# Opening of a two-layer diffusion backbone kernel: conditions and x loaded first, x divided by its rms in place, modulation weights split by VectorE and GpSimd

## The chip, the core and the metric

The kernel runs on one NeuronCore of a Trainium2 chip. Time is device microseconds of one execution, and what is compared is the median of several runs. A profiled execution has a span of its own, from the first to the last instruction in the trace. Engines: TensorE (PE: matmuls; PEld: its weight loads), VectorE (DVE), ScalarE (ACT), GpSimd (POOL) and SyncE (SP), which issues most of the DMAs.

## The reference

```python
for l in range(DEPTH):                                    # 2 layers, D_MODEL = 1024
    sx1, cx1, gx1, sx2, cx2, gx2 = modulation(c, ada_w[l], ada_b[l])      # silu(c) @ w + b
    sc1, cc1, gc1, sc2, cc2, gc2 = modulation(c_ctx[None, :], ada_w[l], ada_b[l])
    hx = modulate(rms_norm(x, norm1_g[l]), sx1, cx1)      # h * (1 + scale) + shift
    hc = modulate(rms_norm(ctx, norm1_g[l]), sc1, cc1)
    zx = split_in(hx @ w_in[l])      # conv a, b | q, k, v | sgu u, v | gates
    ...                              # conv module, window attention, sgu, gated merge, w_o, conv FFN
```

x has 512 rows, ctx has 256, and both have 1024 features. Everything is float32, and the output is compared with a float32 reference.

## The kernel before

Activations are kept transposed: features on partitions, 768 tokens (512 of x, 256 of ctx) along the free axis, eight tiles of 128 features. To keep float32 precision on TensorE at a one-pass rate, an operand is split in two parts of the reduced type fp32r, `hi` (a rounded copy, made by ScalarE in `acopy`) and `lo` (the rest, subtracted by VectorE in `tt`), and a product is hi·hi + hi·lo + lo·hi: three matmuls (`linear_steps`). A plain fp32 matmul needs no split, and the trace shows it as two records.

The opening, up to the first of these products, does four things. (1) `load_cond` brings in c and c_ctx and applies SiLU. (2) `ada_start` computes what the first normalisation needs of the modulation of layer 0, 2048 columns, in two halves `g2`. A half reads 8 row tiles of 128 x 1024 (`k` = 0 to 7), each as two DMAs of 128 x 512; the 128 x 512 tile is the moving operand and the 4 columns of silu(c), silu(c_ctx) (hi and lo) are the stationary one. The result, 4 x 512 in two PSUM tiles `x`, is copied by ScalarE, turned to columns by 8 tiny matmuls against `sel`, and added to the bias into `mods`. Half 0 serves feature tiles 0 to 3, half 1 tiles 4 to 7. Five of the 16 row tiles go through TensorE as plain fp32, eleven are split. (3) `load_x` brings in x and ctx (tiles named g in the trace), four DMAs laid between the row tiles; `rms_sq` sums squares, `rstd_diag` gets 1/rms by a Newton iteration on 128 x 6 numbers and writes it on a diagonal, and `bcast_diag` spreads it over the partitions into PSUM tile `S`. (4) After both halves `norm_mod` makes the eight pairs (hi, lo) of the normalised input, tiles named h: a product with `S` on VectorE, scale and shift on ScalarE, hi and lo.

Then the main stream begins with the first 144 matmuls of layer 0, `ab(0)`: three token parts of 256, two weight tiles, eight feature tiles, three matmuls each. The next product begins with 128 x 512 matmuls.

What sets the order: the kernel is written against a framework that orders each engine's instructions when the program is built, by program order and by priorities (`tc.high_priority`); `paced` adds an order-only dependency on the last matmul noted in `last[0]`. On the chip each engine's queue is strictly in that order. Eight semaphores serve the DMAs in turn, so a DMA is issued only when the one eight places before it has landed.

Of the kernel before, what the change touches and what calls it, by code (L numbers as in the profile page):

```python
# [8 lines left out]
F32 = mybir.dt.float32  # L9
# [9 lines left out]
D = 1024  # L19
# [60 lines left out]
def body(tc, I, out):  # L80
# [136 lines left out]
    acopy(identr, msk[:, :128])  # L217
    acopy(maskb[:, 256:640], msk[:, 128:512])
# [60 lines left out]
    def load_cond():  # L279

        st = T(xp_, [128, 16], F32, "st", 1)
        rw = T(xp_, [2, 1024], F32, "rw", 1)
        nc.scalar.dma_start(out=st[:, :2 * KD], in_=I["ccol"])
        nc.scalar.dma_start(out=rw[:2], in_=I["crow"])
# [3 lines left out]
        act(out=rw[:2], in_=rw[:2], func=AF.Silu)  # L288
        V.memset(silf, 0.0)
        V.tensor_copy(out=silf[:, :, 0:2], in_=st[:, :2 * KD].rearrange("p (k c) -> p k c", c=2))  # L290
        split(silr[:, :, 0:2], silr[:, :, 2:4], silf[:, :, 0:2])
        tt(sel, ident[:4, 0:2], ident[:4, 2:4], add)
        nc.scalar.dma_start(out=sd, in_=rw[:2])

    def ada_start():

        for g2 in range(2):
            pm = [x_ps(), x_ps()]
            for k in range(KD):
                w = [(page("h", 16) if i else page("m", 8))[:, :512] for i in range(2)]  # L300
                for i in range(2):
                    nc.sync.dma_start(out=w[i], in_=I["ada0"][g2, k, :, i * 512:i * 512 + 512])
                for i in range(2):
                    if k < (3, 2)[g2]:
                        nc.tensor.matmul(pm[i][:4], silf[:, k, :], w[i], start=(k == 0), stop=(k == 7))
                        continue
                    hi = page("y", 8, F32R)[:, :512]
                    lo = T(sp, [128, CW0], F32R, "cy", 8)[:, :512]
                    split(hi, lo, w[i])
                    nc.tensor.matmul(pm[i][:4], silr[:, k, :], hi, start=(k == 0), stop=False)  # L310
                    nc.tensor.matmul(pm[i][:4], silr[:, k, :], lo, start=False, stop=(k == 7))
                yield
            with tc.high_priority(offset=600):
                pt = c_ps()
                for i, g in enumerate((g2, g2 + 2)):
                    r = page("t", NTP)[:4, :512]
                    acopy(r, pm[i][:4])
                    for j in range(4):
                        c = (i * 4 + j) * 2
                        nc.tensor.matmul(pt[:, c:c + 2], r[:, j * 128:j * 128 + 128], sel, start=True, stop=True)  # L320
                pv = pt[:, :16].rearrange("p (j c) -> p j c", c=2)
                for c in range(2):
                    for i, g in enumerate((g2, g2 + 2)):
                        tt(mods[0][c][:, g * 4:g * 4 + 4], pv[:, i * 4:i * 4 + 4, c], adab[0][:, g * 4:g * 4 + 4], add)
            yield
# [134 lines left out]
    def linear_steps(res, w, cs, hs, segs, k0=0):  # L460
# [3 lines left out]
        for o, n, c in segs:  # L464
            p = acc_ps(c)[:, :n]
            for k in range(nk):
                hi, lo = hs[k0 + k]
                nc.tensor.matmul(p, w[0][:, k, cs], hi[:, o:o + n], start=(k == 0), stop=False)  # L468
# [65 lines left out]

    load_cond()
    fvs[0] = load_fv(0)
    ag = ada_start()

    def ada_steps(n):
        for _ in range(n):  # L540
            next(ag, None)

    ada_steps(4)
    xs = load_x(lambda i: ada_steps(2))
# [4 lines left out]
    with tc.high_priority(offset=1000):  # L549
        bcast_rstd(acc, 0, NT, 1.0 / D, bx)  # L550
    ada_steps(99)
    px.close()
    hs = h_pages()
    for c in range(2):
        a1 = mod_scale(0, c, 1, FV_N1)
        for o, n, c_ in parts_of(True):
            if c_ == c:
                norm_mod(xs, bx[:, o:o + n], hs, o, n, a1, mods[0][c][:, 0:8])

    for l in range(2):  # L560
# [78 lines left out]
        def ab(i, w, t, sg_):  # L639
            for p, o, n, c in linear(w[0], slice(0, 128), hs, sg_):  # L640
                with evac():
                    act(out=t[:, o:o + n], in_=p, func=AF.Copy)
            for p, o, n, c in linear(w[1], slice(0, 128), hs, sg_):
# [5 lines left out]
        def ab_load(i):  # L649
            if i == 0 and full:  # L650
                ab_load.raw = [raw_tile() for _ in range(2)]
                for h in range(2):
                    for b in range(2):
                        nc.sync.dma_start(
                            out=ab_load.raw[b].rearrange("p (k c) -> p k c", k=8)[:, :, h * 128:h * 128 + 128],
                            in_=I["w_in"][l, :, b * 512 + h * 128:b * 512 + h * 128 + 128].rearrange("(k p) c -> p k c", p=128))
# [598 lines left out]
```

## Time and profile before

| what | us |
|---|---|
| median of 3 runs | 2097.68 (2093.98 to 2099.98) |
| profiled execution, its time | 2097.33 |
| profiled execution, its span | 2095.5 |
| TensorE busy in the span | 2050.4 (98%) |
| first matmul of the main stream | 51.43 |
| first 128 x 512 matmul behind the first product | 72.64 |

The page gives busy time by engine, the costliest groups of instructions and the DMAs. The views by stretch (windows) and in order of time (timeline) are read for the first 80 us and at the border between the layers. A row of the timeline has its start, its length, the engine and line, output and inputs, their shape, the count of instructions merged in it and, in brackets, the idle time before it and what ended that.

### The profile page before, as it was taken

How to read it: one execution, taken by the hardware profiler on the slowest of the kernel's cores; microseconds unless marked ns; L12 is line 12 of the kernel's file. 1: busy time of each engine (PE TensorE's matmuls, PEld its weight loads, DVE VectorE, ACT ScalarE, POOL GpSimd, SP SyncE). 2: the span in 40 equal slices, each digit the busy share in tenths (PEclk: the TensorE clock that was granted, in tenths of full speed). 3: DMA queues.
4: the chain of work that ended last, by engine and by line, in shares of the span. 5: the costliest groups of instructions: out<-in, count | busy, mean ns of one | idle time of the engine just before them, and what ended most of it. 6: DMA issues, size and time to landing. Idle time of an engine off the chain costs nothing.

```text
span 2095.5 us, 29640 instructions
## 1 busy us (share of the span) xinstructions
PE 2050.4 (98%) x11628; PEld 1769.3 (84%) x11628; DVE 1564.9 (75%) x3134; ACT 894.4 (43%) x1485; POOL 10.6 (1%) x24
## 2 busy tenths in 40 slices
PE   6999999999999899999999999999999999999999
PEld 2888898888878898888888898879888888888887
DVE  5689888888667778867595768998987467655654
ACT  5532235677523453323232325433687335333331
POOL 0000000000000000000000000000000000000000
PEclk9999999999999999999999999999999999999999
DMA  8121112213576133444343422322212432222321
GB/s 279 57 81 61 61 61 76 86 55 105 153 220 203 65 101 124 139 141 150 102 141 101 161 78 91 121 65 77 75 46 63 124 126 93 89 92 96 106 99 62
DMA packets 160468, 221.39 MB, mean 106 GB/s; under 512 B 7364, under 2 KB 102340, under 8 KB 160328
## 3 DMA queue, kind: packets, MB, share of 16 engines
q1 hardware_dynamic: 155712, 212.89, 31.5%
q10 hardware_dynamic: 4616, 6.61, 1.0%
q8 instruction: 91, 1.49, 0.3%
q14 instruction: 49, 0.40, 0.1%
HBM read 215.27 MB, written 4.20 MB: 105 GB/s over the span
## 4 chain that ended last, share of the span: by engine, by line
PE 59%; DVE 7%; DMA 4%; ACT 2%; issue 1%; SPq 0%; ACTq 0%; DVEq 0%
PE x L469 8%; PE x L468 8%; PE x L470 8%; PE b L469 7%; PE b L468 7%; PE b L470 7%; DMA t<-in_adat 2%; DVE cy L120 2%; DVE hl L117 2%; PE S L470 2%; PE S L468 2%; PE S L469 2%; PE c L470 2%; PE c L469 2%; PE c L468 2%
## 5 line engine op out<-in xcount | busy, mean ns | idle before, releaser
L114 ACT ACTIVATE hl<-raw 128x1024 fp32r<-128x1024 f32 x264 | 279.2, 1059 | 497.9 <-PE c L469 184.4
L117 DVE TENSOR_TENSOR hl<-raw,hl 128x1024 fp32r<-128x1024 f32 x264 | 322.5, 1222 | 158.8 <-ACT hl L114 156.0
L468 PE MATMUL x<-h,hl 128*128 128x512 f32 (+1 forms) x760 | 292.7, 387 | 6.6 <-ACT h L114 6.6
L470 PE MATMUL x<-h,hl 128*128 128x512 f32 (+1 forms) x760 | 291.7, 385 | 1.4 <-DVE hl L117 1.4
L469 PE MATMUL x<-h,hl 128*128 128x512 f32 (+1 forms) x760 | 292.6, 386 | 0.0
L120 DVE SCALAR_TENSOR_TENSOR cy<-cy,fv 128x503 f32<-128x503 f32 (+29 forms) x240 | 208.5, 880 | 3.0
L469 PE MATMUL b<-h,hl 128*128 128x512 f32 (+1 forms) x552 | 203.9, 370 | 0.0
L468 PE MATMUL b<-h,hl 128*128 128x512 f32 (+1 forms) x552 | 203.5, 370 | 0.0
L470 PE MATMUL b<-h,hl 128*128 128x512 f32 (+1 forms) x552 | 203.2, 369 | 0.3 <-DVE hl L117 0.3
L468 PEld LDWEIGHTS x<-h,hl 128*128 128x128 f32 x760 | 145.3, 192 | 31.0 <-ACT h L114 7.3
L470 PEld LDWEIGHTS x<-h,hl 128*128 128x128 f32 x760 | 145.5, 192 | 27.7 <-DVE hl L117 2.4
L469 PEld LDWEIGHTS x<-h,hl 128*128 128x128 f32 x760 | 145.9, 192 | 23.4 <-DVE h L117 0.3
L470 PEld LDWEIGHTS b<-h,hl 128*128 128x128 f32 x552 | 104.2, 189 | 18.1 <-DVE hl L117 0.7
L468 PEld LDWEIGHTS b<-h,hl 128*128 128x128 f32 x552 | 104.2, 189 | 17.0
L469 PEld LDWEIGHTS b<-h,hl 128*128 128x128 f32 x552 | 104.2, 189 | 16.4
L468 PE MATMUL c<-h,hl 128*128 128x256 f32 x400 | 112.7, 282 | 0.1
L469 PE MATMUL c<-h,hl 128*128 128x256 f32 x400 | 112.5, 281 | 0.1
L470 PE MATMUL c<-h,hl 128*128 128x256 f32 x400 | 112.5, 281 | 0.0
L120 DVE SCALAR_TENSOR_TENSOR m<-b,ff,m 128x511 f32<-128x511 f32 (+2 forms) x118 | 80.8, 688 | 36.1 <-ACT m L1128 34.6
L114 ACT ACTIVATE y<-m 128x512 fp32r<-128x512 f32 (+1 forms) x51 | 36.4, 713 | 128.3 <-DVE m L117 121.8
L468 PE MATMUL b<-y,hl 128*128 128x512 f32 (+1 forms) x256 | 86.3, 338 | 0.7 <-ACT y L114 0.7
L470 PE MATMUL b<-y,hl 128*128 128x512 f32 (+1 forms) x256 | 85.8, 335 | 0.0
(338 smaller groups left out, 4983.0 us busy)
## 6 DMA issues: line engine op xcount, KB each, us to landing
t<-in_adat SPq DMA_DIRECT2D x200, 256.0 KB, 3.4
raw<-in_w_in SPq DMA_DIRECT2D x44, 1024.0 KB, 5.3
raw<-in_ffn_up SPq DMA_DIRECT2D x44, 1024.0 KB, 5.1
raw<-in_ffn_down SPq DMA_DIRECT2D x22, 1024.0 KB, 5.1
raw<-in_w_o SPq DMA_DIRECT2D x8, 1024.0 KB, 7.3
g<-in_xt SPq DMA_DIRECT2D x8, 768.0 KB, 5.5
m<-in_ada SPq DMA_DIRECT2D x16, 256.0 KB, 5.4
h<-in_ada SPq DMA_DIRECT2D x16, 256.0 KB, 5.8
```

The lines of the kernel that those rows point to most:

```text
L114: act(out=o, in_=i, func=AF.Copy)
L117: V.tensor_tensor(out=o, in0=a, in1=b, op=op)
L120: return V.scalar_tensor_tensor(out=o, in0=a, scalar=s, in1=b, op0=op0, op1=op1)
L468: nc.tensor.matmul(p, w[0][:, k, cs], hi[:, o:o + n], start=(k == 0), stop=False)
L469: nc.tensor.matmul(p, w[0][:, k, cs], lo[:, o:o + n], start=False, stop=False)
L470: last[0] = nc.tensor.matmul(p, w[1][:, k, cs], hi[:, o:o + n], start=False, stop=(k == nk - 1))
```

## The change

The conditions come over SP's queue ahead of all else and x right behind them, before any modulation weight. Each half (`ada_half`) still has 8 row tiles; two of half 0 (k = 0, 1) and three of half 1 (k = 5 to 7) are plain fp32. In a split, ScalarE makes hi as before, and lo is subtracted by VectorE for the left half of a row tile and by GpSimd for the right one. 1/rms is found while half 0 runs, its spreading stands behind row tile 4 of half 0, and x is multiplied by it in place, eight products of 128 x 768. With half 0 known, `scaled_tiles` makes feature tiles 0 to 3: hi and the full value each by an own ScalarE instruction from x, lo by VectorE. Tiles 4 to 7 follow half 1, with hi on ScalarE and the full value on VectorE. The first weights `w_in` (`raw0`) are requested behind all modulation weights, and `behind` (in both layers) holds the first product's matmuls behind the last matmul written before them.

```diff
-    def ada_start():
-        for g2 in range(2):
...
-                    if k < (3, 2)[g2]:
...
-                    split(hi, lo, w[i])
...
+        nc.sync.dma_start(out=st[:, :2 * KD], in_=I["ccol"])
+        nc.sync.dma_start(out=rw[:2], in_=I["crow"])
...
+    def ada_half(g2, between=None):
+        pm = [x_ps(), x_ps()]
+        cyp = lambda: T(sp, [128, CW0], F32, "cy", 8)[:, :512]
+        src = [lambda: page("m", 8)[:, :512], lambda: page("y", 8)[:, :512], cyp, lambda: page("m", 8)[:, :512]]
+        tag, bufs = (("h", 16), ("y", 8))[g2]
+        for k in range(KD):
+            w = [src[g2 * 2 + k // 4]() for i in range(2)]
+            for i in range(2):
+                nc.sync.dma_start(out=w[i], in_=I["ada0"][g2, k, :, i * 512:i * 512 + 512])
+            for i in range(2):
+                if (k >= 5 if g2 else k < 2):
+                    last[0] = nc.tensor.matmul(pm[i][:4], silf[:, k, :], w[i], start=(k == 0), stop=(k == 7))
+                    continue
+                hi, lo = (page(tag, bufs, F32R)[:, :512] for _ in range(2))
+                acopy(hi, w[i])
+                (nc.gpsimd if i else V).tensor_tensor(out=lo, in0=w[i], in1=f(hi), op=sub)
+                nc.tensor.matmul(pm[i][:4], silr[:, k, :], hi, start=(k == 0), stop=False)
+                last[0] = nc.tensor.matmul(pm[i][:4], silr[:, k, :], lo, start=False, stop=(k == 7))
+            if between:
+                between(k)
...
+                stt(a1[c][:, v], mods[0][c][:, 8 + g2 * 4:12 + g2 * 4], 1.0, fvs[0][:, FV_N1 + g2 * 4:FV_N1 + g2 * 4 + 4], add, mul)
...
+                r = nc.tensor.matmul(p, w[0][:, k, cs], hi[:, o:o + n], start=(k == 0), stop=False)
+                if behind and k == 0:
+                    paced(r)
...
+    def scaled_tiles(js, o, n, c):
+        v = slice(o, o + n)
+        for j in js:
+            hi, lo = hs[j]
+            t = page("t", NTP)
+            aff = dict(in_=xs[j][:, v], func=AF.Identity, scale=a1[c][:, j:j + 1], bias=mods[0][c][:, j:j + 1])
+            act(out=hi[:, v], **aff)
+            if j < 4:
+                act(out=t[:, :n], **aff)
+            else:
+                ts(t[:, :n], xs[j][:, v], a1[c][:, j:j + 1], mul, mods[0][c][:, j:j + 1], add)
+            tt(lo[:, v], t[:, :n], f(hi[:, v]), sub)
...
-    ada_steps(4)
-    xs = load_x(lambda i: ada_steps(2))
+    xs = load_x()
...
+        dg = rstd_diag(acc, 0, NT, 1.0 / D)
+    ada_half(0, lambda k: k == 4 and bcast_diag(dg, NT, bx))
+    for j in range(KD):
+        tt(xs[j], xs[j], bx[:, :NT], mul)
+    hs = h_pages()
+    scaled_tiles(range(4), 0, NX, 0)
+    ada_half(1)
+    raw0 = [raw_tile() for _ in range(2)]
...
+    scaled_tiles(range(4), NX, NC, 1)
+    for q in parts_of(True):
+        scaled_tiles(range(4, 8), *q)
     px.close()
-    hs = h_pages()
-    for c in range(2):
...
-                norm_mod(xs, bx[:, o:o + n], hs, o, n, a1, mods[0][c][:, 0:8])
```

ScalarE's queue before, at the end of half 1: the last copy of a modulation tile (y from h), the copies of the result (t from x), the split of the first weights (hl from raw), two small loads, and the first steps of the normalised input (t and h).

```order
L114 ACTIVATE y<-h 128x512
L114 ACTIVATE t<-x 4x512 x2
L114 ACTIVATE hl<-raw 128x1024 x2
L240 DMA lng<-in_sln 128x512
L240 DMA lnb<-in_sln 128x512
L452 ACTIVATE t<-t,mod_85,a_429 128x256 x2
L114 ACTIVATE h<-t 128x256
```

The modulation came first, the weight split and the normalised input behind it. ScalarE's queue now, from half 0's result (t from x) over the making of feature tiles 0 to 3 (h and t from g) into half 1 (y from cy):

```order
L114 ACTIVATE t<-x 4x512 x2
L549 ACTIVATE h<-g_110,mod_83,a_108 128x512
L551 ACTIVATE t<-g_110,mod_83,a_108 128x512 x2
L551 ACTIVATE t<-g_111,mod_83,a_108 128x512 x2
L549 ACTIVATE h<-g_110,mod_84,a_109 128x256
L549 ACTIVATE h<-g_110,mod_83,a_108 128x512
L114 ACTIVATE y<-cy 128x512
L549 ACTIVATE h<-g_111,mod_83,a_108 128x512
L114 ACTIVATE y<-cy 128x512
```

and the end of the same queue's half 1:

```order
L549 ACTIVATE h<-g_111,mod_84,a_109 128x256
L114 ACTIVATE y<-cy 128x512
L114 ACTIVATE hl<-raw 128x1024
L114 ACTIVATE y<-cy 128x512
L114 ACTIVATE hl<-raw 128x1024
L114 ACTIVATE y<-m 128x512 x2
L114 ACTIVATE t<-x 4x512 x2
```

Twelve instructions on feature tiles 0 to 3 and the two weight splits now stand ahead of the last copies of half 1.

TensorE's queue before, from the last split tile (x from cy) over the result of half 1 (c from sel) and the spreading of 1/rms (S) to the first main matmuls (x and b from h and hl):

```order
L311 MATMUL x<-cy,silr 4x512
L320 MATMUL c<-sel,t 128x2 x4
L435 MATMUL S<-t,ones 128x512
L435 MATMUL S<-t,ones 128x256
L320 MATMUL c<-sel,t 128x2 x4
L468 MATMUL x<-h,hl 128x256
```

and now, from the end of half 1 (split tiles of y, plain tiles of m) to the first main matmuls (x from h and hl):

```order
L313 MATMUL x<-y,silr 4x512 x2
L314 MATMUL x<-y,silr 4x512
L308 MATMUL x<-m,silf 4x512
L314 MATMUL x<-y,silr 4x512
L308 MATMUL x<-m,silf 4x512 x5
L324 MATMUL c<-sel,t 128x2 x4
L473 MATMUL x<-h,hl 128x256
```

The six plain tiles of half 1 stand behind its last split tile, where plain tiles were the first of each half, and S is spread earlier, within half 0.

## Rows read from the trace of the kernel before

**Rows 1.** The page: busy time of TensorE, its share of the span and its instructions.

```profile
PE 2050.4 (98%) x11628; PEld 1769.3 (84%) x11628; DVE 1564.9 (75%) x3134; ACT 894.4 (43%) x1485; POOL 10.6 (1%) x24
```

**Rows 2.** Windows of 10 us: start and end, length, busy us of each engine (instructions), granted clock of TensorE, DMA share, GB/s.

```profile
0.00:10.00 10.00, 1.90 (x3) 0.35 (x4) 1.11 (x6) 4.56 (x7) 0.21 (x4) 1.00 0.82 256
10.00:20.00 10.00, 9.07 (x22) 1.79 (x20) 4.41 (x8) 3.78 (x6) 0.00 (x0) 1.00 1.00 363
20.00:30.00 10.00, 8.29 (x32) 2.82 (x32) 6.53 (x12) 8.94 (x13) 0.00 (x0) 1.00 1.04 400
30.00:40.00 10.00, 7.31 (x24) 3.56 (x25) 7.58 (x17) 7.42 (x14) 0.00 (x0) 0.70 1.10 335
```

**Rows 3.** Timeline of TensorE in the opening: plain fp32 tiles (L305), split tiles (L310, L311), sums of squares (L422), result of half 1, spreading of 1/rms (L435), main stream (L468 to L470).

```profile
9.76 1.91 PE L305 MATMUL x<-h,silf 128*4 128x512 f32 x2
11.46 1.91 PE L305 MATMUL x<-m,silf 128*4 128x512 f32 x2
...
18.06 0.40 PE L311 MATMUL x<-cy,silr 128*4 128x512 f32 x1
18.29 0.39 PE L310 MATMUL x<-y,silr 128*4 128x512 f32 x1
...
25.77 1.02 PE L305 MATMUL x<-m,silf 128*4 128x512 f32 x2
26.63 1.02 PE L305 MATMUL x<-h,silf 128*4 128x512 f32 x2
...
33.95 2.72 PE L422 MATMUL b<-ones,t 128*128 128x1 f32 x12
...
44.16 0.40 PE L311 MATMUL x<-cy,silr 128*4 128x512 f32 x1 [0.29 <-DVE cy L117]
...
45.47 1.56 PE L435 MATMUL S<-t,ones 128*128 128x512 f32 x4
...
51.43 0.58 PE L468 MATMUL x<-h,hl 128*128 128x256 f32 x1 [3.43 <-ACT h L114]
...
58.03 0.28 PE L470 MATMUL b<-h,hl 128*128 128x256 f32 x1
58.15 0.28 PE L468 MATMUL b<-h,hl 128*128 128x256 f32 x1
...
72.64 0.40 PE L468 MATMUL x<-h,hl 128*128 128x512 f32 x1
```

**Rows 4.** Timeline of ScalarE in the opening: squares (L414), hi copies and copies of the result (L114), scale and shift (L452).

```profile
25.15 3.90 ACT L414 ACTIVATE t<-g 128x768 f32<-128x768 f32 x5
...
34.20 0.62 ACT L114 ACTIVATE y<-m 128x512 fp32r<-128x512 f32 x1
34.72 0.61 ACT L114 ACTIVATE y<-h 128x512 fp32r<-128x512 f32 x1
...
43.67 0.59 ACT L114 ACTIVATE t<-x 4x512 f32<-4x512 f32 x1 [4.81 <-PE x L311]
...
45.09 1.99 ACT L114 ACTIVATE hl<-raw 128x1024 fp32r<-128x1024 f32 x2
...
51.29 0.58 ACT L452 ACTIVATE t<-t,mod,a 128x256 f32<-128x256 f32 x1
51.78 0.40 ACT L114 ACTIVATE h<-t 128x256 fp32r<-128x256 f32 x1
52.09 0.59 ACT L452 ACTIVATE t<-t,mod,a 128x256 f32<-128x256 f32 x1
```

**Rows 5.** Timeline of VectorE: lo subtraction of a modulation tile and the small step behind it, the diagonal of 1/rms, the lo of the first weights, the additions into mods, the product with S; then, at the border between the layers, the first step of the Newton iteration on 128 x 2 numbers and the diagonal that follows it.

```profile
38.22 0.68 DVE L117 TENSOR_TENSOR cy<-m,y 128x512 fp32r<-128x512 f32 x1
38.82 0.15 DVE L117 TENSOR_TENSOR nut<-nyt 128x6 f32<-128x6 f32 x1
...
44.02 0.95 DVE L117 TENSOR_TENSOR t<-identr,nyt 128x768 f32<-128x768 f32 x1
...
46.16 1.23 DVE L117 TENSOR_TENSOR hl<-raw,hl 128x1024 fp32r<-128x1024 f32 x1 [1.09 <-ACT hl L114]
48.04 0.37 DVE L117 TENSOR_TENSOR mod<-c,adab 128x4 f32<-128x4 f32 x4 [0.65 <-PE c L320]
...
49.53 1.41 DVE L117 TENSOR_TENSOR t<-g,S 128x256 f32<-128x256 f32 x4
...
1267.75 0.16 DVE L126 TENSOR_SCALAR nvt<-b 128x2 f32<-128x2 f32 x1 [0.30 <-PE b L422]
...
1270.72 0.42 DVE L117 TENSOR_TENSOR t<-identr,nyt 128x256 f32<-128x256 f32 x1
```

**Rows 6.** Windows of 1 us, TensorE alone: busy us (instructions), granted clock, DMA share, GB/s.

```profile
40.00:41.00 1.00, 1.00 (x4) 0.63 1.06 295
...
50.00:51.00 1.00, 0.00 (x0) 0.99 0.92 289
...
57.00:58.00 1.00, 1.00 (x7) 0.59 0.00 0
```

**Rows 7.** DMA issues of the first 80 us: the first weights, with count, KB each, median us from issue to landing.

```profile
raw<-in_w_in SPq DMA_DIRECT2D x4, 512.0 KB, 7.7
```

**Rows 8.** Timeline of TensorE at the border between the layers.

```profile
1264.26 0.39 PE L470 MATMUL x<-h,hl 128*128 128x256 f32 x1 [0.87 <-DVE hl L117]
```

**Rows 9.** GpSimd's groups by shape: its memsets of 64 x 512.

```profile
L915 POOL MEMSET qT<- 64x512 f32 x20 | 10.4, 521 | 1569.7 <-PE b L732 892.6 <-PE b L731 236.8 <-PE S L940 181.4
```

More of the change, by code (lines that the diff above doesn't have):

```diff
@@ L291, in load_cond @@
         split(silr[:, :, 0:2], silr[:, :, 2:4], silf[:, :, 0:2])
+        act(out=rw[:2], in_=rw[:2], func=AF.Silu)
+        nc.scalar.dma_start(out=sd, in_=rw[:2])
+        acopy(identr, msk[:, :128])
+        acopy(maskb[:, 256:640], msk[:, 128:512])
         tt(sel, ident[:4, 0:2], ident[:4, 2:4], add)
-        nc.scalar.dma_start(out=sd, in_=rw[:2])
-    def ada_start():
-        for g2 in range(2):
[L298 to L303, printed above, removed]
-                    if k < (3, 2)[g2]:
[L305 to L308, printed above, removed]
-                    split(hi, lo, w[i])
[L310 to L314, printed above, removed]
-                for i, g in enumerate((g2, g2 + 2)):
[L316 to L321, printed above, removed]
-                for c in range(2):
-                    for i, g in enumerate((g2, g2 + 2)):
-                        tt(mods[0][c][:, g * 4:g * 4 + 4], pv[:, i * 4:i * 4 + 4, c], adab[0][:, g * 4:g * 4 + 4], add)
-            yield
@@ new lines, in ada_half @@
+    def ada_half(g2, between=None):
[18 more added lines that the diff above has]
+                between(k)
+        with tc.high_priority(offset=600):
+            pt = c_ps()
+            for i, g in enumerate((g2, g2 + 2)):
+                r = page("t", NTP)[:4, :512]
+                acopy(r, pm[i][:4])
+                for j in range(4):
+                    c = (i * 4 + j) * 2
+                    nc.tensor.matmul(pt[:, c:c + 2], r[:, j * 128:j * 128 + 128], sel, start=True, stop=True)
+            pv = pt[:, :16].rearrange("p (j c) -> p j c", c=2)
+            for c in range(2):
+                for i, g in enumerate((g2, g2 + 2)):
+                    tt(mods[0][c][:, g * 4:g * 4 + 4], pv[:, i * 4:i * 4 + 4, c], adab[0][:, g * 4:g * 4 + 4], add)
+                v = slice(g2 * 4, g2 * 4 + 4)
+                stt(a1[c][:, v], mods[0][c][:, 8 + g2 * 4:12 + g2 * 4], 1.0, fvs[0][:, FV_N1 + g2 * 4:FV_N1 + g2 * 4 + 4], add, mul)
@@ L458, in norm_mod, with linear_steps @@
             tt(lo[:, v], t[:, :n], f(hi[:, v]), sub)
-    def linear_steps(res, w, cs, hs, segs, k0=0):
+    def linear_steps(res, w, cs, hs, segs, k0=0, behind=False):
         nk = w[0].shape[1]
@@ L533, in load_x @@
         return [xs[j // 2][:, (j % 2) * 768:(j % 2) * 768 + 768] for j in range(8)]
+    def scaled_tiles(js, o, n, c):
[10 more added lines that the diff above has]
+            tt(lo[:, v], t[:, :n], f(hi[:, v]), sub)
     load_cond()
     fvs[0] = load_fv(0)
[L537 to L541, printed above, removed]
-    ada_steps(4)
-    xs = load_x(lambda i: ada_steps(2))
+    a1 = [T(cp, [128, 8], F32, "a0%d1" % c, 1) for c in range(2)]
+    xs = load_x()
     acc = page("t", NTP)
@@ L650, in ab_load @@
             if i == 0 and full:
[L651 to L656, printed above, removed]
+                ab_load.raw = raw0
             elif i % 2 == 0:
```

21 lines of the change are left out of this document (7 added, 14 removed).

## The prediction

> **What bounds the kernel now.** The page first: TensorE is busy for 98% of the span [rows 1], so nearly all that is left to win lies where it isn't dense, and the windows show that this is the opening [rows 2]. The timeline of TensorE gives the two marks [rows 3]: the main stream starts at 51.43 and its first product ends at 72.64, where the 128 x 512 matmuls begin. From there the queues are the same before and after except at the layer border, and TensorE sets the pace. So the change is worth what it moves the 72.64, plus the border. The opening ended with half 1: its last lo matmul at 44.16, then the result, S, and the normalised input; the stream's first matmul waited 3.43 us for ScalarE's h [rows 3].
>
> **The change, step by step.** It adds and removes hardly any matmuls (ten plain tiles either way), so what counts is which queue is last. I follow the chain in the new order with durations from rows; all new clock times are estimates.
>
> *x lands, about 13.2.* x is 3.15 MB and 0.4 MB of small loads travel with it. By 10 us 2.56 MB had moved (256 GB/s), the next stretch ran at 363 [rows 2]; with a part of the next tile on the way that is 3.7 MB, 13.2. At 400 GB/s throughout it would be 11.5, with a slower start 14.
>
> *1/rms, about 22.9.* A square takes 0.78 (3.90 for five) [rows 4]: two remain after the last x tile, 14.8; the last addition, a 128 x 768 like the diagonal, 0.95 [rows 5], with hand-over 16.0. Six fp32 matmuls took 2.72 at the lower clock [rows 3]: 18.7. The Newton chain took 2.97 at the border (1267.75 to 1270.72), with one foreign instruction in it as now [rows 5]: with a slightly longer one 21.9. Diagonal 0.95: 22.9.
>
> *S, about 27.0.* The spreading stands behind three plain tiles and six split ones. A plain tile takes 0.86 at 2.4 GHz (25.77 to 26.63) and 1.70 at half of it (9.76 to 11.46) [rows 3]; I take 4.1 for three (bounds 2.6 and 5.1): 22.8. Six split tiles of two matmuls at 0.23 (18.06 to 18.29) [rows 3]: 25.6. The spreading took 1.56 [rows 3]: 27.0.
>
> *Half 0 known, about 32.9.* VectorE multiplies x by S. Four 128 x 256 took 1.41 [rows 5], 0.35 each, so 0.88 for 768 columns; between the first two pieces stand two lo of 0.60 (38.22 to 38.82) [rows 5]. The last lo is done at 30.0, TensorE at 30.6, two copies of 0.59 [rows 4], eight tiny matmuls and the additions (0.37 for four) [rows 5]: 32.9. This hides nothing and is hidden by nothing: ScalarE has run dry by then.
>
> *ScalarE's queue, 14.2 us.* From here to the last hi of half 1 the queue holds, in order, work of three kinds. Scale and shift on 256 columns is followed after 0.49 (51.29 to 51.78), a plain copy on 256 after 0.31 (51.78 to 52.09), one on 512 after 0.52 (34.20 to 34.72) [rows 4]; so scale and shift on 512 is 0.70. Eight of these (hi and full value of four tiles) 5.6; four on ctx 2.0; nine copies of modulation tiles 4.7; two weight splits, 1.99 together [rows 4]. Sum 14.2, end 47.1. The transfers don't hold it: by the rates of [rows 2] the modulation has landed near 35 and the first half of the weights (7.7 us from issue) [rows 7] near 38. VectorE runs beside it and ends with the second weight lo (1.23) [rows 5] and the last modulation lo: 48.0. GpSimd's last subtraction ends about there. No row shows a two-operand GpSimd instruction; its one-output memset of half the partitions takes 0.52 [rows 9], and three streams at that rate would be 1.56. I take 1.1, between them; at either end it is covered by the plain tile ahead of its matmul.
>
> The Trainium skill, GPSIMD Engine Reference, section Performance versus the Vector engine, gives 4497 ns for a two-operand instruction of 2048 columns; a quarter of it, 1.1 us, is an estimate for 512. The sum would not move by it.
>
> *Six plain tiles at the end, about 8.* Before, plain tiles led each half. Now all six of half 1 are behind the last split tile. At 2.4 GHz they take 5.2, at 1.2 GHz 10.2. TensorE was granted half its clock when it had idled 3.4 us before the main stream, from 51.0 to 57.6 [rows 3, 6], and in the new order it has only some 18 short matmuls between 32 and 48, so I take about 6 us at the lower clock: 8.0. With the last lo matmul, half 1 is through at 56.3, against 44.6 before.
>
> *From there to the end of the first product, 24.5.* Before it was 28.1 (44.6 to 72.64). Feature tiles 0 to 3 are ready now. The result takes two copies, the tiny matmuls and the additions, 2.1; ScalarE first makes four full values of ctx (2.0), then two hi for each tile, 0.98 a tile: VectorE has the fourth lo of the first part at 7.2. By then 24 of 144 matmuls are done; 120 at 0.12 (58.03 to 58.15) [rows 3] are 14.4. A gap of 5 us with little work costs the clock again, some 2.9. Bounds 21.6 and 27. End 80.8.
>
> *Sum.* 80.8 against 72.64 is +8.2. At the layer border the first product's matmuls no longer run ahead of their weights' lo, a wait of 0.87 [rows 8], and nothing is late in its place: −0.9. Span 2095.5 + 7.3 = 2102.8. The profiled execution's time was 1.8 above its span and 0.35 under the median of 2097.68: 2105.
>
> **Rivals.** *The transfers end it.* If half 0's result reached ScalarE by 26 us in place of 32.9, the queue would wait for weights at the end, not work. Then: weights near 38.2, split and two copies 2.0, GpSimd 1.1, plain tiles at the full clock 5.2, 21.6 more: 68.1, −4.5 − 0.9, 2092. For it speaks that 400 GB/s are seen from 20 us on [rows 2]; against it, that with each step of the 1/rms chain at its lower bound I get only to 28.7. This is the case on the other side; its deciding point is that 26 us.
>
> *The clock stays up.* The same chain to 48.0, but the plain tiles at 2.4 GHz (53.6) and no second loss (21.6): 75.2, +2.6 − 0.9, 2099.4. For it: 0.23 matmuls with waits between them ran at the full clock from 16 to 24 [rows 3]. Against: the idle before 51.43 cost it, and the new queue is emptier.
>
> *VectorE and GpSimd hold each other up.* Five subtractions of half 1 run while VectorE does nearly nothing but two-operand instructions. If each waits for the other, 1.1 to 1.56 five times, less 1 us of slack of VectorE against ScalarE, is about 5, with some 1 in half 0: 2111. No row before has both engines at work, so none speaks for or against. The Trainium skill, GPSIMD Engine Reference, section Specifications, says that GpSimd's SBUF interfaces are shared with VectorE and contend with VectorE instructions that have two SBUF inputs, which would make this the likely one; by that rule VectorE, not ScalarE, would be last in half 1.
>
> **How the numbers follow.** Chances: the forecast 0.41, transfers 0.15, clock 0.24, contention 0.20. A measurement of this kernel can tell about 0.3%, 6.3 us, so slower means above 2104.0 and faster below 2091.4. The forecast's own range is 2100 to 2109, with some 0.26 of its 0.41 beyond 2104.0; contention adds 0.19 of its 0.20: slower 0.45. What the forecast leaves (0.15), nearly all of the clock case (0.23) and a third of the transfers' case (0.05) are within 0.3%: 0.43. Faster is the rest of the transfers' case and 0.02 of the others, 0.12. Lowest and highest bounds of all steps give 2095.6 and 2111; the range is 2094 to 2112, which leaves out most of the transfers' case and the upper part of contention.
>
> **What would show it.** In the new trace: x's last square near 14.8; S near 27; the first scale and shift near 33; a ScalarE queue without idle from there to the last hi copy near 47; TensorE's plain tiles from 48 with a granted clock of 0.50; the first 128 x 512 matmul near 81. If ScalarE waits for a DMA late in half 1, the first rival holds; if VectorE's lo subtractions are longer than 0.69 while GpSimd works, the third. The forecast is wrong if half 0's result comes before 28 us, or if the scale and shift on 512 columns is much below 0.70.

## The result and the profile after

The changed kernel took 2117.33 us (median of five runs; 2115.18 to 2118.24) against 2097.68 (five runs; 2093.98 to 2099.98) of the kernel before: a ratio of 1.0099, with a 95% interval of 1.0086 to 1.0112. It is slower, as forecast, but by about 20 us and not by 7, and 2117.33 lies outside the range of 2094 to 2112. The profiled execution has a span of 2116.2 us (before 2095.5).

The first view is the timeline of TensorE in the changed kernel, which answers to [rows 3]. Columns: start, us, engine, line, operation, tiles, shape, count, and in brackets the idle time before it and what ended it.

```profile
14.63 1.86 PE L308 MATMUL x<-m,silf 128*4 128x512 f32 x2 [14.63 <-DMA m<-in_ada]
17.95 2.72 PE L427 MATMUL b<-ones,t 128*128 128x1 f32 x12 [1.46 <-DVE t L117]
...
30.11 1.45 PE L440 MATMUL S<-t,ones 128*128 128x512 f32 x4
...
37.05 1.56 PE L324 MATMUL c<-sel,t 4*128 4x2 f32 x8
43.93 0.59 PE L314 MATMUL x<-y,silr 128*4 128x512 f32 x1 [5.32 <-DVE y L312]
...
56.83 1.87 PE L308 MATMUL x<-m,silf 128*4 128x512 f32 x2
...
59.15 5.51 PE L308 MATMUL x<-m,silf 128*4 128x512 f32 x10
...
65.56 0.39 PE L473 MATMUL x<-h,hl 128*128 128x256 f32 x1
...
90.34 0.40 PE L473 MATMUL x<-h,hl 128*128 128x512 f32 x1
```

The two marks: the main stream starts at 65.56 (before 51.43) and the first 128x512 matmul stands at 90.34 (before 72.64). So 17.70 of the 20.7 us of span are lost in the opening. Half 1 is through at 64.66 (59.15 + 5.51) where it was through at 44.6. TensorE stood idle for 5.32 us ahead of the first lo of half 1, while weights and hi were there.

The windows of TensorE in the changed kernel (us from:to, length, busy time with count, granted clock as a share, DMA share, GB/s) answer to [rows 2]. From 40 to 60 the clock was 0.50, that is 1.2 GHz, and by 62 it was back at 2.4 GHz: the plain tile at 56.83 and the first of the five from 59.15 ran at the lower clock, the rest at the full one. The transfers were over by 50, so they don't end the opening.

```profile
30.00:40.00 10.00, 7.53 (x35) 0.87 1.13 332
40.00:50.00 10.00, 4.63 (x10) 0.50 0.14 36
50.00:60.00 10.00, 7.59 (x15) 0.50 0.01 2
60.00:70.00 10.00, 9.15 (x39) 0.84 0.01 4
...
61.00:62.00 1.00, 1.00 (x4) 0.85 0.00 0
```

ScalarE in the same stretch, against [rows 4]: it has half 0's result to work with from 39.11, and then makes scale, shift, copies and the weight splits without a gap up to 53.40 (52.26 + 1.14), that is 14.3 us.

```profile
13.88 1.70 ACT L419 ACTIVATE t<-g 128x768 f32<-128x768 f32 x2 [0.30 <-DMA g<-in_xt]
...
35.11 1.06 ACT L114 ACTIVATE t<-x 4x512 f32<-4x512 f32 x2 [4.75 <-PE x L314]
39.11 0.81 ACT L549 ACTIVATE h<-g,mod,a 128x512 fp32r<-128x512 f32 x1 [2.94 <-DVE a L120]
...
52.26 1.14 ACT L114 ACTIVATE y<-m 128x512 fp32r<-128x512 f32 x2
63.83 0.59 ACT L114 ACTIVATE t<-x 4x512 f32<-4x512 f32 x1 [10.44 <-PE x L308]
```

VectorE, against [rows 5]. The seven additions of squares start only at 10.58, behind a wait of 5.84 us for the vectors fv. The steps of the Newton iteration on 128x6, and the subtractions, come in a short and a long form: 0.17 and 1.2 us, 0.69 and up to 1.75 us.

```profile
10.20 0.18 DVE L124 TENSOR_SCALAR fv<-fv 128x32 f32<-128x32 f32 x1 [5.84 <-DMA fv<-in_fv]
...
10.58 7.31 DVE L117 TENSOR_TENSOR t<-t 128x768 f32<-128x768 f32 x7
20.71 0.16 DVE L126 TENSOR_SCALAR nvt<-b 128x6 f32<-128x6 f32 x1 [2.81 <-PE b L427]
...
21.34 1.25 DVE L124 TENSOR_SCALAR nvt<-nvt 128x6 f32<-128x6 f32 x1
22.50 0.15 DVE L117 TENSOR_TENSOR nut<-nyt 128x6 f32<-128x6 f32 x1
22.69 1.20 DVE L117 TENSOR_TENSOR nut<-nut,nvt 128x6 f32<-128x6 f32 x1
...
24.20 0.69 DVE L312 TENSOR_TENSOR h<-m,h 128x512 fp32r<-128x512 f32 x1
...
25.80 0.96 DVE L117 TENSOR_TENSOR t<-identr,nyt 128x768 f32<-128x768 f32 x1
26.68 1.75 DVE L312 TENSOR_TENSOR h<-m,h 128x512 fp32r<-128x512 f32 x1
...
38.91 0.16 DVE L120 SCALAR_TENSOR_TENSOR a<-mod,fv 128x4 f32<-128x4 f32 x1
...
51.14 3.44 DVE L117 TENSOR_TENSOR hl<-raw,hl 128x1024 fp32r<-128x1024 f32 x2
54.51 1.75 DVE L312 TENSOR_TENSOR y<-m,y 128x512 fp32r<-128x512 f32 x1
```

GpSimd in the same kernel:

```profile
18.58 2.61 POOL L312 TENSOR_TENSOR h<-m,h 128x512 fp32r<-128x512 f32 x2 [18.13 <-ACT h L114]
21.26 2.61 POOL L312 TENSOR_TENSOR h<-y,h 128x512 fp32r<-128x512 f32 x2
...
29.91 1.27 POOL L312 TENSOR_TENSOR h<-y,h 128x512 fp32r<-128x512 f32 x1 [2.03 <-DMA m<-in_ada]
...
53.47 2.23 POOL L312 TENSOR_TENSOR y<-m,y 128x512 fp32r<-128x512 f32 x1
```

The two views belong together. GpSimd's pair from 21.26 has its first end near 22.56 and its second at 23.87. The long steps of VectorE end at 22.59 and 23.89: a step of 0.17 us that starts while GpSimd subtracts ends when GpSimd's instruction does. The step at 20.71, which reads TensorE's result b, is the exception: it took 0.16 in the middle of GpSimd's first pair. The other way round, GpSimd takes 1.27 us at 29.91, where VectorE is idle, and 2.23 at 53.47, where VectorE works through the first weights.

### The profile page after: what moved, and what is told of

It reads as the page before. It is cut to its first block, busy times and chain, and to the rows that moved or that the text cites. A ratio compares the mean times of both kernels' runs of the same rounds, so it can differ in the third digit from the quotient of the medians.

```text
span 2116.2 us, 29636 instructions
## 1 busy us (share of the span) xinstructions
PE 2057.8 (97%) x11628; PEld 1772.2 (84%) x11628; DVE 1567.0 (74%) x3111; ACT 891.2 (42%) x1470; POOL 26.9 (1%) x35
## 4 chain that ended last, share of the span: by engine, by line
PE 78%; DVE 12%; DMA 5%; ACT 3%; issue 2%; SPq 0%; ACTq 0%; DVEq 0%
PE x L476 10%; PE x L477 10%; PE x L473 10%; PE b L476 8%; PE b L473 8%; PE b L477 8%; DMA t<-in_adat 3%; PE c L477 2%; PE c L476 2%; PE c L473 2%; DVE cy L120 2%; DVE hl L117 2%; PE b L998 2%; PE S L473 2%; PE S L476 2%; PE S L477 2%
## 5 line engine op out<-in xcount | busy, mean ns | idle before, releaser
L114 ACT ACTIVATE hl<-raw 128x1024 fp32r<-128x1024 f32 x264 | 279.3, 1059 | 495.3 <-PE c L476 188.4
L120 DVE SCALAR_TENSOR_TENSOR m<-b,ff,m 128x511 f32<-128x511 f32 (+2 forms) x118 | 80.8, 688 | 36.3 <-ACT m L1146 34.8
L473 PE MATMUL x<-y,hl 128*128 128x512 f32 (+1 forms) x224 | 82.0, 366 | 3.1 <-DVE g L120 3.1
```

What stands on the lines that cost most here:

```text
L114: act(out=o, in_=i, func=AF.Copy)
L120: return V.scalar_tensor_tensor(out=o, in0=a, scalar=s, in1=b, op0=op0, op1=op1)
L473: r = nc.tensor.matmul(p, w[0][:, k, cs], hi[:, o:o + n], start=(k == 0), stop=False)
```

## The experiments

All are compared with the kernel before. "End of the first product" is the start of the first 128x512 matmul in the timeline of TensorE, the mark that stood at 72.64.

| kernel | end of the first product, us | median, us | ratio to before (95%) |
|---|---|---|---|
| before | 72.64 | 2097.68 | 1 |
| changed | 90.34 | 2117.33 | 1.0099 (1.0086 to 1.0112) |
| e1, no GpSimd | 84.87 | 2112.44 | 1.0088 (1.0074 to 1.0102) |
| e2, plain rows first | 85.45 | 2110.66 | 1.0076 (1.0063 to 1.0089) |
| e3, half 1 first | 84.72 | 2112.10 | 1.0083 (1.0069 to 1.0097) |
| e4, order in layer 0 only | 90.48 | 2114.79 | 1.0091 (1.0077 to 1.0105) |
| e5, e1 to e4 together | 81.61 | 2104.41 | 1.0032 (1.0018 to 1.0045) |
| e6, fv on GpSimd | 90.36 | 2119.59 | 1.0128 (1.0112 to 1.0144) |
| e8, TensorE kept busy | 88.18 | 2113.13 | 1.0081 (1.0066 to 1.0096) |
| e9, half 0 ahead of x | 84.66 | 2111.03 | 1.0072 (1.0060 to 1.0084) |
| e10, e9 with e1, e2, e4 | 80.64 | 2102.96 | 1.0028 (1.0017 to 1.0039) |
| e11, before with x first | 71.59 | 2095.99 | 1.0005 (0.9995 to 1.0014) |
| e12, e11 and x divided early | 77.75 | 2102.29 | 1.0038 (1.0025 to 1.0051) |
| e13, the same behind half 1's lo | 75.95 | 2099.22 | 1.0022 (1.0013 to 1.0031) |
| e14, e11 with the scale ahead | 71.17 | 2096.37 | 1.0005 (0.9994 to 1.0016) |
| e15, e11 and GpSimd | 76.00 | 2100.04 | 1.0024 (1.0016 to 1.0032) |

The kernel before had medians of 2094.38 to 2097.68 beside these, so kernels are compared by their ratios, and what moves inside the opening by the mark. Against the changed kernel the ratios tell e5, e9 and e10 apart (their intervals lie below 1.0086); those of e1 to e4 and of e8 overlap with its own, so what these gain rests on the mark, which is read from one execution of each. The changed kernel and e4, whose openings have the same instructions, have marks of 90.34 and 90.48.

### Taking parts out of the changed kernel

**e1**, all subtractions on VectorE:

```diff
-                (nc.gpsimd if i else V).tensor_tensor(out=lo, in0=w[i], in1=f(hi), op=sub)
+                tt(lo, w[i], f(hi), sub)
```

> Every lo subtraction of the modulation weights on VectorE, none on GpSimd. If the two engines hold each other up (theory): VectorE's instructions go back to their lengths of before (lo about 0.65 us in place of 1.24, the Newton steps on 128x6 about 0.15 in place of 1.25), half 0 is known 2 to 3 us earlier although VectorE has six more subtractions there, half 1's last lo is 2 us earlier, and the end of the first product is 3 to 5 us earlier than with the change as it is: about 2113 us. If GpSimd only takes load off VectorE (rival): eleven more instructions of about 0.6 us on VectorE, of which those of half 0 lie on the chain: 4 to 6 us later, about 2122 us.

The first product ended 5.47 us earlier, although VectorE had eleven more subtractions. In its timeline all steps are short:

```profile
20.59 0.17 DVE L124 TENSOR_SCALAR nvt<-nvt 128x6 f32<-128x6 f32 x1
...
22.28 0.69 DVE L117 TENSOR_TENSOR h<-m,h 128x512 fp32r<-128x512 f32 x1
```

The theory holds in size, but not in all its places: half 0 was known at 38.2, only 0.8 earlier, although S was spread 2.5 us earlier: the additional subtractions stand there among the multiplications by S. The gain came from half 1: through at 60.14 (the plain tiles end there) in place of 64.66. Of this, 2.8 us are VectorE's last lo (done at 53.45, in the changed kernel at 56.26), and 1.7 are the plain tiles, which took 5.7 us in place of 7.4: TensorE's clock was at 1.00 from 55 on, in the changed kernel only from 62. So part of what GpSimd costs comes by way of the clock.

**e2**, half 1's plain rows first:

```diff
-                if (k >= 5 if g2 else k < 2):
+                if k < (2, 3)[g2]:
```

> In half 1 the three plain rows are the first and not the last (the number of plain tiles stays). If the six plain tiles at the low clock behind the last split tile cost what the prediction gave them (theory): they move into TensorE's idle time from about 38 to 44 us, and the end of the first product comes 6 to 9 us earlier than with the change as it is, about 2109.5 us. ScalarE's and VectorE's queues then end with the last split tile somewhat later, since they no longer finish three rows before the end: this takes back up to 2 us. Rival, transfers: the last split rows are now the last weights to land; if these land after 45 us, the gain falls under 3 us, about 2115 us.

4.89 us earlier, below the 6 to 9 of the theory: the plain tiles moved to 39.67 to 46.4, but one of them came between half 0's two groups of tiny matmuls (half 0 known 1.1 later), and the last lo came from VectorE at 57.9, not at 56.3. The transfers were not in the way.

**e3**, ScalarE's tile work behind half 1:

```diff
-    scaled_tiles(range(4), 0, NX, 0)
     ada_half(1)
+    scaled_tiles(range(4), 0, NX, 0)
```

> The scale and shift of feature tiles 0 to 3 (image columns) stand behind half 1 in the program, not ahead of it. Theory of the queue (ScalarE's 14.2 us of work between half 0's result and half 1's last hi copy is what makes half 1 late, and half 1 need not wait for half 0's result at all): half 1's last hi copy comes before 40 us in place of 53.4, half 1 is through near 50 in place of 64.6; the scale and shift of all eight tiles then follows, about 6 us of it uncovered; net 8 to 12 us earlier, about 2107 us. Rival (the work is only moved behind, and TensorE has nothing to do meanwhile): within 3 us of the change as it is, 2114 to 2120 us.

ScalarE's last hi copy of half 1 ended at 47.0 (before the edit 53.4), half 1's result was copied at 53.92 in place of 63.83, 10 us earlier. The first product gained 5.62: ScalarE then stood idle for 5.02 us up to that copy, and afterwards made nearly all scale and shift from 55.27 to 69.64 in one piece. The theory was right about half 1 and too high about the net.

**e4**, the order on the first product in layer 0 only:

```diff
-            for p, o, n, c in linear(w[0], slice(0, 128), hs, sg_, behind=i == 0):
+            for p, o, n, c in linear(w[0], slice(0, 128), hs, sg_, behind=full and i == 0):
...
```

> The order set on the first matmuls of the first product (behind the matmul before them) only in layer 0, so that the layer border stands as in the kernel before. If that order is what costs the border its time in the trace after (about +0.6 us net, in place of the 0.9 us gained that the prediction took): 0.6 us earlier, about 2116.7 us, and the wait at 1270 to 1300 us for VectorE's diagonal is gone. Rival (the border's change is an effect of where the stream happens to stand): no difference, 2117.3 us; either is below what the interval can tell, so the trace decides.

The opening is the same (90.48). At the border the wait for VectorE's g is gone and those of [rows 8] are back. The waits of TensorE, summed by line and releaser, first of the changed kernel from 1260 to 1345 us:

```profile
PE c L473 <- DVE g L120: 1.9, 1, 1.9
```

and of e4 from 1258 to 1342:

```profile
PE x L477 <- DVE hl L117: 0.9, 1, 0.9
PE b L477 <- DVE hl L117: 0.3, 1, 0.3
```

If the matmuls of both traces are numbered from the end and set side by side, e4 gains 1.3 us across the border (2.08 us ahead at 1282, 3.38 at 1439). So in this pair of traces the order costs there, where the prediction took a gain of 0.9. The same comparison shows e4 1.8 to 2.1 us ahead by 690 to 757, where both kernels have the same instructions in the same order on TensorE: two executions differ by so much in that stretch, which is more than the 1.3.

**e5**, e1 to e4 together.

> x first as in the changed kernel, with the four edits tried so far together: all subtractions on VectorE, half 1's plain rows first, scale and shift of tiles 0 to 3 behind half 1, the order on the first product in layer 0 only. Alone they took 5.5, 4.9, 5.6 and 0 us off the end of the first product and some 2 us later on. If they are separate costs: 14 to 16 us off the end of the first product, about 2099 us. If they are the same wait seen from three queues (rival): 6 to 9 us off, about 2106 to 2109 us.

8.73 us off the opening: the rival's 6 to 9. Alone, e1 to e3 took off 16.0 in sum, so their costs overlap: largely one wait, seen from three queues.

**e6**, the vectors fv scaled by GpSimd:

```diff
-        ts(fv[:, FV_GB:FV_LB + 4], fv[:, FV_GB:FV_LB + 4], 0.5, mul)
...
+        e = V if l else nc.gpsimd
+        e.tensor_scalar(out=fv[:, FV_GB:FV_LB + 4], in0=fv[:, FV_GB:FV_LB + 4], scalar1=0.5, scalar2=None, op0=mul)
...
```

> The changed kernel, with the two small scalings of the layer's vectors (128x32 and 128x124) done by GpSimd, so that VectorE does not wait for their transfer ahead of the additions of squares. Theory (the 5.8 us for which VectorE waits until 10.2 delay the sum of squares and with it S and half 0): the last addition ends 1 to 2 us earlier, at 16 to 17, and the first product 1 to 2 us earlier than in the changed kernel, about 2115.5 us. Rival (S is not what half 0's result waits for): the additions end earlier and nothing else moves, 2117 us.

The rival: the additions ended at 17.19 in place of 17.89, and the mark did not move (90.36), since the Newton iteration then met GpSimd at work in three steps and not in two. The time was even 0.3% higher than the changed kernel's, while its profiled span was 0.4 us shorter; that is not explained.

**e8**, TensorE kept busy:

```diff
+        bp = b_ps() if g2 else None
...
+                for _ in range(((24 if (k, i) == (0, 0) else 4) if g2 else 0)):
+                    r = nc.tensor.matmul(bp[:, :128], ones, ones, start=True, stop=True)
+                    paced(r)
+                    last[0] = r
                 hi, lo = (page(tag, bufs, F32R)[:, :512] for _ in range(2))
```

> The changed kernel with matmuls added that compute nothing: ones by ones, 128x128 fp32, into a result that nobody reads, 24 ahead of half 1's first split tile and 4 ahead of each further one, so that TensorE is not idle while it waits for half 1's subtractions. If the lower clock is a cost of its own (theory; the six plain tiles took 8.3 us where 5.2 stand for the full clock, and the first product starts at half the clock): the granted clock stays near 1.0 from 38 to 62 us, the end of the first product comes 3 to 5 us earlier than in the changed kernel, about 2113 us against 2117. If waits alone set the end (rival): the plain tiles get shorter but the time stays within 1.5 us of the changed kernel's.

The windows of TensorE in e8 show the full clock from 38 us on, 2.4 GHz:

```profile
44.00:50.00 6.00, 5.41 (x41) 1.00 0.00 1
50.00:56.00 6.00, 5.45 (x42) 1.00 0.00 0
56.00:60.00 4.00, 4.00 (x18) 1.00 0.01 4
...
68.00:72.00 4.00, 3.03 (x10) 0.59 0.44 124
```

The plain tiles took 5.31 us in place of 7.4, and the mark came 2.16 us earlier, less than the 3 to 5 expected: the first product met the lower clock again (0.59 from 68 to 72), when it waited for VectorE's h. The clock is a cost of its own here, of some 2 us.

**e9**, half 0's weights ahead of x:

```diff
+    ada_half(0)
     xs = load_x()
...
-    ada_half(0, lambda k: k == 4 and bcast_diag(dg, NT, bx))
+        bcast_diag(dg, NT, bx)
```

> The changed kernel with half 0's weights loaded ahead of x and worked on at once, as in the kernel before; x follows, then half 1's weights. Split by both engines, plain tiles, division by the rms in place and the early scale and shift stay. If loading x first is the main cost (theory: half 0's result is known at 39 us because its weights come behind x and its lo stand in VectorE's queue among the steps for 1/rms, and nothing of ScalarE's tile work can start before it): half 0 is known near 22, S near 38, half 1's result near 50, and the first product ends at 72 to 76 in place of 90: 15 us earlier, about 2101 us. If the order of loading is of no matter and the queues behind it are what costs (rival): S and the scaled tiles come later by as much as half 0 comes earlier, and the time is within 5 us of the changed kernel's, 2112 or more.

Half 0 was known at 24.1, 15 us earlier; but S was spread at 42.84, 12.7 us later. VectorE of e9, where the seven additions took 8.27 us and not 7.31, the last of them beside GpSimd:

```profile
23.94 0.16 DVE L120 SCALAR_TENSOR_TENSOR a<-mod,fv 128x4 f32<-128x4 f32 x1
24.02 8.27 DVE L117 TENSOR_TENSOR t<-t 128x768 f32<-128x768 f32 x7
...
45.44 6.14 DVE L117 TENSOR_TENSOR g<-g,S 128x768 f32<-128x768 f32 x7 [1.33 <-PE S L440]
```

The scale and shift needs both, and began at 46.43 on ScalarE. The mark gained 5.68 us, the time came out at 2111, next to the rival's 2112 and 10 us above the theory's. Loading order only chooses which of the two comes second.

**e10**, e9 with the edits of e1, e2 and e4.

> Half 0's weights ahead of x as in the experiment before it in this list, and with it all subtractions on VectorE, half 1's plain rows first, and the order on the first product in layer 0 only. If the costs found so far are separate: 3 to 6 us below the experiment before it, the first product ends near 69, about 2095 us, level with the kernel before or up to 5 us under it. Rival (VectorE, with all subtractions and the eight multiplications by S, becomes the last queue): as that experiment or slower, 2100 us or more.

The mark lies 4.02 us below e9's, as in the theory, but not near 69, and the time, 2103, is above the rival's 2100: in VectorE's queue the eight multiplications by S (38.85 to 45.85) stood ahead of half 1's lo, for which TensorE waited 7.05 us.

### Putting parts into the kernel before

**e11**, x first and nothing else:

```diff
-    ada_steps(4)
-    xs = load_x(lambda i: ada_steps(2))
+    xs = load_x()
```

> The kernel before with one thing changed: the four tiles of x are loaded ahead of all modulation weights, not in between them. VectorE makes all lo, the plain rows lead each half, the scale and shift follow both halves, GpSimd has nothing. If x first is no cost in itself (theory: the transfers end at the same time either way, and what costs in the changed kernel is what its queues then do with the weights: ScalarE's tile work ahead of half 1's copies, plain rows last, two engines that hold each other up): half 1 is through at 44 to 47 us and the first product ends within 3 us of the 72.64 of before, 2094 to 2100 us. If loading x first is itself what makes half 1 late (rival: TensorE and both other engines have nothing to do with weights for the first 14 us, and that work is missing at the end): half 1 through after 50, the first product ends 6 us later or more, 2103 us or more.

The theory: no difference (0.9995 to 1.0014), the mark at 71.59. VectorE's timeline of e11 shows half 1's last lo done at 44.36, though VectorE waited 4.82 us in the middle, for half 0's tiny matmuls:

```profile
37.36 0.37 DVE L117 TENSOR_TENSOR mod<-c,adab 128x4 f32<-128x4 f32 x4 [4.82 <-PE c L320]
37.65 0.68 DVE L117 TENSOR_TENSOR cy<-h,y 128x512 fp32r<-128x512 f32 x1
...
43.67 0.69 DVE L117 TENSOR_TENSOR cy<-h,y 128x512 fp32r<-128x512 f32 x1
```

**e12**, and x divided by its rms in place:

```diff
         bcast_rstd(acc, 0, NT, 1.0 / D, bx)
+    for j in range(KD):
+        tt(xs[j], xs[j], bx[:, :NT], mul)
     ada_steps(99)
...
```

> As the experiment before it in this list, and x is divided by its rms in place (eight multiplications of 768 columns on VectorE, 7 us) as soon as S is there, ahead of half 1's subtractions; the scale and shift behind both halves then read x itself. Theory: the seven us stand in VectorE's queue ahead of half 1's lo and make half 1 late by 3 to 6 us, more than the 1.4 us that they save behind it: 3 us slower than that experiment, about 2100 us. Rival (VectorE catches up, since the weights come slower than it splits them): 1 to 2 us faster than that experiment, about 2095 us.

The theory, and more: the mark 6.16 us later than e11. Six of the multiplications (37.51 to 42.77 in VectorE's timeline) stand ahead of half 1's subtractions, which begin at 42.70 and end at 52.27, where e11 ends them at 44.36.

```profile
37.51 5.26 DVE L117 TENSOR_TENSOR g<-g,S 128x768 f32<-128x768 f32 x6
```

**e13**, the multiplications yield to half 1:

```diff
+    ada_steps(17)
     for j in range(KD):
         tt(xs[j], xs[j], bx[:, :NT], mul)
     ada_steps(99)
...
```

> As the experiment before it in this list, but the eight multiplications yield to half 1's subtractions in VectorE's queue. Theory: half 1 is through as early as without them, and the scale and shift starts 1.5 to 3 us earlier than in the kernel before because the first tiles are divided already: the first product ends near 70, 2092 to 2096 us, the best of all. Rival (four multiplications that stand behind the last subtraction hold up half 1's result or the first weights' lo): no better than the kernel before.

The rival: half 1's last subtraction ends at 45.83, but behind it five multiplications and the first weights' two lo stand in VectorE's queue ahead of the small operation that makes the scale. It runs at 53.69, in e11 at 48.80; the mark is 75.95.

**e15**, e11 and every second subtraction on GpSimd:

```diff
-                    split(hi, lo, w[i])
+                    if i:
+                        acopy(hi, w[i])
+                        nc.gpsimd.tensor_tensor(out=lo, in0=w[i], in1=f(hi), op=sub)
+                    else:
+                        split(hi, lo, w[i])
```

> The kernel before with x loaded first (which alone made no difference) and, with it, the changed kernel's split: GpSimd makes the lo of the second tile of each row, VectorE of the first. Here VectorE is last in half 1 (subtractions back to back from 37.65 to 44.3), so GpSimd takes half of the last queue. If the two engines hold each other up (theory): a pair of subtractions takes 1.3 to 2 us as in the changed kernel, against 1.2 for two on VectorE alone; half 1 is through 1 to 3 us later and the first product ends at 72 to 75 against 71.59: 2096 to 2100 us. If GpSimd relieves VectorE where VectorE is the bound (rival): half 1 is through 2 us earlier, the first product ends near 69, about 2093 us.

The theory, and a little more: the mark 4.41 us later than e11, 1.0024 (1.0016 to 1.0032) against 1.0005 (0.9995 to 1.0014). VectorE, then GpSimd, then TensorE of e15:

```profile
24.34 1.22 DVE L126 TENSOR_SCALAR nyt<-ntt 128x6 int32<-128x6 int32 x1
...
25.59 1.23 DVE L117 TENSOR_TENSOR nut<-nyt 128x6 f32<-128x6 f32 x1
26.85 1.19 DVE L117 TENSOR_TENSOR nut<-nut,nvt 128x6 f32<-128x6 f32 x1
27.96 0.68 DVE L117 TENSOR_TENSOR cy<-m,y 128x512 fp32r<-128x512 f32 x1
...
38.37 5.85 DVE L117 TENSOR_TENSOR cy<-m,y 128x512 fp32r<-128x512 f32 x5
```

```profile
20.93 7.08 POOL L311 TENSOR_TENSOR cy<-h,y 128x512 fp32r<-128x512 f32 x5 [20.48 <-ACT y L114]
36.61 5.86 POOL L311 TENSOR_TENSOR cy<-h,y 128x512 fp32r<-128x512 f32 x4 [8.60 <-ACT y L114]
```

```profile
28.69 0.40 PE L315 MATMUL x<-cy,silr 128*4 128x512 f32 x1 [2.62 <-DVE cy L117]
```

The price was paid in half 0: TensorE waited 2.62 us for a lo (27.96) that stood in VectorE's queue behind the held steps, and 0.60 for the next one. Half 1 was through 3.2 us later than in e11 (48.05 against 44.80). Plain tiles met the lower clock in both kernels, in e15 from 38 to 41, in e11 from 24 to 25. From 32.65 to 47.65 TensorE waited for neither engine, so e15 does not show what the pair costs when it is the last queue. Side by side in half 1, VectorE's five subtractions took 5.85 us, in which GpSimd made some three (an estimate, since its first of the four ran ahead of them). On VectorE alone eight, 0.60 each as in e11, would be 4.8.

**e14**, e11 with the small operation for the scale at the priority of half 1's result:

```diff
+    with tc.high_priority(offset=600):
+        a01 = [mod_scale(0, c, 1, FV_N1) for c in range(2)]
...
```

> The kernel before with x loaded first, and the two small operations that make the scale (a) given the same priority as half 1's result, so that they don't stand behind the second subtraction of the first weights (1.22 us) in VectorE's queue. Theory: the scale and shift starts 1 us earlier, the first product ends near 70.5, 2094 to 2095 us, 1 us below the kernel with x first alone. Rival (the first weights' lo is then late by the same 1.2 us for the second matmul): no difference, 2096 us.

0.42 us at the mark, nothing that the time shows. No kernel tried here is faster than the kernel before.

## Why the prediction was right in sign and too small

By its own chain, with what the changed kernel's trace shows (differences of 9.5 us against the 80.8 of the forecast):

- *x lands, sum of squares done 16.0*: 17.89. The last square ended at 15.58 (forecast 14.8), and the additions, 1.04 each back to back from 10.58, were behind it. The wait for fv was in the queue, and the prediction did not see it. +1.9. It mattered less than it looks: without it the additions ended 0.7 earlier, and nothing behind them moved (e6).
- *1/rms 6.9 us later*: 8.9, to 26.76. Two of the Newton steps took 1.25 and 1.20 in place of 0.17. +2.0. (The chain at the border, from which the forecast took its length, has two foreign instructions in it, at 1268.69 and 1270.14, and not one.)
- *S 4.1 us later*: 4.8. The spreading stood behind a lo that VectorE began at 26.68 and that took 1.75 beside GpSimd; TensorE waited 2.35 us for it. +0.7.
- *Half 0 known 5.9 us after S*: 7.5, to 39.07. The lo among the multiplications by S ended as forecast, 3.1 us after S. The two groups of tiny matmuls came one behind the other and took from 35.75 to 38.61, the second as the clock fell (0.70 from 37 to 38). +1.6.
- *ScalarE's queue 14.2 us*: 14.3. Right, and so was its place: no idle time from 39.11 to 53.40.
- *VectorE's last lo 0.9 behind it*: 2.9, to 56.26. The first weights' two lo took 3.44 us, where the prediction had 1.23 each, and the last 1.75. +2.0.
- *Half 1 through 8.3 us later*: 8.4. Right in sum, partly by luck: the lower clock lasted only to about 61.3, not for 6 us of plain tiles, and these took 7.4 in place of 8.0, but two lo matmuls of 0.5 each stood in the same stretch, where the forecast had one of 0.3.
- *To the end of the first product 24.5*: 25.7. +1.2.

The step that failed is the one on which the prediction had no row: it took GpSimd's subtraction as 1.1 us "covered by the plain tile ahead of its matmul", put its effect on VectorE at nothing, and gave the two engines that hold each other up a rival of 0.20. They do. GpSimd's subtraction took 1.27 us alone and up to 2.23 beside VectorE, and the waits that come of it make up some 4.7 of the 9.5 us above (Newton steps 2.0, S 0.7, the last lo 2.0). Taking GpSimd out (e1) brought the mark forward by 5.5, some of it through the clock, and putting its split alone into another kernel (e15) put the mark back by 4.4 and made that kernel slower. The rival's price, 6 us, was right in size but not in place: it put 1 us of it into half 0, where 2.7 were paid. With the 6 added to the forecast the mark would have been near 87. The other 4.8 of the 9.5 are the sum of squares, the tiny matmuls and the way from half 1 to the end of the first product. The Trainium skill, SBUF — State Buffer, section Who interferes with whom, states that VectorE and GpSimd share a pair of ports as an exclusive lock, that a VectorE instruction with two inputs in SBUF or in a two-port mode contends for it with a GpSimd instruction that reads SBUF, and that whoever issues first holds the pair for the whole instruction while the other is blocked. The trace agrees: the steps held at 21.34 and 22.69 end at 22.59 and 23.89, where GpSimd's two instructions end (21.26 to 23.87), and a step of 0.17 that is held pays the whole rest of GpSimd's 1.3.

What the runs say of the other steps: loading x first was cleared (e11: 1.0005, 0.9995 to 1.0014). Of the eight multiplications by S the prediction priced only those on the way to half 0's lo; all eight, put into e11, cost 6.2 us (e12), since they stand ahead of half 1's subtractions. ScalarE's early tile work and the plain rows at the end each cost about 5 us when taken out of the changed kernel (e3, e2), and the three together 8.7 (e5): they overlap, so no list of parts adds up to 17.7. The clock is some 2 of it (e8). Even e5, without the three, ends its first product 9.0 us later than the kernel before; it still has the eight multiplications, but no run takes them out of it. Of the rivals, that the clock stays up and that the transfers end it were wrong: the clock was at 0.50 from 40 to 60, and the transfers were done long before the last lo.

Behind the opening the prediction gave −0.9, and the trace has +3.0 (20.7 − 17.7). With the matmuls of the traces before and after numbered from the end, the changed kernel is late by 17.7 at 90, by about 16.9 from 120 to 590, by 19.8 at 760, and goes from 20.0 to 20.6 across the border. So the border's term has the wrong sign, +0.6; without the order on layer 1's first matmuls it is 1.3 less, in one pair of traces (e4). Most of the rest, 2.9, is lost in the stretch from 590 to 760. Two executions with the same instructions there, the changed kernel and e4, differ by about 2, so it has no cause that these runs show.

## What to carry to other kernels

Giving a second engine half of a queue pays only if the two don't share what they wait for: measure one pair side by side before you count on it, and look at the short instructions around it, which pay most. Work that is "ready early" is not free on an in-order engine: ask what stands behind it, and whether that is the end of the stage. When several queues end near each other, taking one cost out shows only the distance to the next, so try a part both ways, out of the new kernel and into the old one.

## What was not expected of the hardware

The smallest instructions paid most: a VectorE step of 128x6 elements, 0.17 us by itself, took 1.19 to 1.25 us when it began while GpSimd subtracted two 128x512 tiles. A step that read TensorE's result was not held (0.16, at 20.71). GpSimd's own subtraction took 1.27 us beside an idle VectorE and up to 2.23 beside a busy one. And 20 us at 1.2 GHz cost little: with matmuls put into TensorE's waits (e8) the clock stayed at 2.4 GHz up to 68, but the mark moved by 2.2 us only.
